# Norms of neighbourhood queries and keys: squares split in two parts, products made a piece at a time during the next block

## The chip, the cores and the metric

The kernel runs on one core of one Trainium2 chip. The core has five engines with a queue of instructions each: TensorE (PE in the profile; its weight loads are shown as PEld), VectorE (DVE), ScalarE (ACT), GpSimd (POOL) and SyncE (SP), which here issues nearly all DMAs. The metric is the device time of one execution in microseconds (us), less is better. The clock of TensorE that was granted in the profiled execution is 0.982 of full speed on average.

## The reference

One layer of a hybrid backbone over 1024 latent tokens of 1024 channels and 256 context tokens. After RMSNorm and modulation one input projection feeds two groups: a gated DeltaNet (conv blocks `q`, `k`, `v`, gate `z`; scans in both directions, which need the inverses of small triangular matrices) and a neighbourhood attention with 8 heads of 64 channels. Both outputs are joined, projected, and a SwiGLU network follows. The change touches only the norms of the attention group's queries and keys:

```python
q, k, v = [t.reshape(B, L, NA_HEADS, NA_HEAD_DIM) for t in jnp.split(p, 3, axis=-1)]
q = rms_norm(q, q_norm_w) * NA_HEAD_DIM ** -0.5
k = rms_norm(k, k_norm_w)
```

where `rms_norm` divides by the root of the mean of the squares over the 64 channels of a head (plus 1e-6) and multiplies by a weight per channel.

## The kernel before, in words

Tokens lie along the free axis: T = 1280, context first (`SEGS` cuts them in pieces of 256, 512 and 512; queries need the last two only, 1024 tokens). The input projection is made in blocks of 128 output channels. `Block` is such a block with the channels on the partitions: kinds `q`, `k`, `v` (conv), `nq` and `nk` (attention), four of each. `Wide` is a pair of blocks with the tokens on the partitions (`z`, `nv`), made in tiles of 128 tokens.

Products are three-term: inputs and weights are kept as a high part and the remainder, both in the type fp32r, which PE takes in one pass (`hh`, `hl`; `whi`, `wlo`), and high x high, low x high and high x low are added in PSUM (line 389). For one of the 8 contraction tiles (`KT`) and one term a block has as many matmuls as pieces. Matmuls on plain fp32 data are two instructions each in the trace.

The list `jobs` has the order: `k` 0 to 3 and `nv` half 1, then `nk` 0, 1, 2, `nv` half 0, `nk` 3, `nq` 0, 1, 2, `q` 0 to 3, `z`, `v` 0, `z`, `v` 1 to 3, `nq` 3. In round n of the loop (from line 974 on) the next job's weights are prefetched (a DMA, a cast to `whi` on ACT at line 198, a subtraction to `wlo` on POOL at line 199), job n's matmuls are made, its result is copied out of PSUM (`evac`, line 422 for `nq` and `nk`), then the norm of job n-1 is made (`norm`), and last the squares of job n (`silu`, line 455). Where job n is a `Wide`, the norm of job n-1 is made after its fifth tile.

The norm of an `nk` or `nq` block: for each piece a matmul of the squares `r` with a 128 x 128 matrix of two blocks of ones, `M[C_BD2]`, in plain fp32 (line 476), which sums the squares of a head and spreads the sum over its channels; Ln on ACT out of PSUM (line 477); after the pieces Exp with factor -0.5 (479 for `nq`, 481 for `nk`); a multiplication on DVE (484); a split into two fp16 parts on ACT and DVE (489, 490; 496, 497); four DMAs to DRAM (502). The matmul's result lies in a bank of the tag `m`, of which there are two; the banks of the blocks have the tag `blk`, of which there are four.

Between the contraction tiles and token tiles, `bg.step` runs background work a step at a time: first `block_inverses` (POOL makes `rc` at line 782, PE and ACT make `W` at 795 and 797, DVE multiplies at 802 to 807, PE transposes at 814, DVE eliminates at 824 and 826, PE turns back at 836, the result goes to DRAM as `x_d`), then `preps` (lines 886 to 920), which loads it as `xc`. The first four preps need the context chunks only; the others wait until the `q` blocks are done. From the job `nq` 3 on, attention starts (`sc`, lines 295 to 319), and the scans follow.

The order of instructions in each queue is not the written one: a planner takes the instructions in the written order but moves what its own estimate of times holds ready ahead of what it holds late, and allocates buffers of a tag in turn. A queue works strictly in the order so fixed. The tag `kx` has three buffers of up to 1280 x 4 bytes, used by `hl16`, `vt`, `kT`, `kk`, `kd` and the `z` tiles.

Of the kernel before, what the change touches and what calls it, by code (L numbers as in the profile page):

```python
# [9 lines left out]
F32 = mybir.dt.float32  # L10
F32R = mybir.dt.float32r
# [3 lines left out]
OP = mybir.AluOpType  # L15
# [4 lines left out]
D, L, CT, T = 1024, 1024, 256, 1280  # L20
# [13 lines left out]
C_ID, C_LE, C_GE, C_BD2, C_ONE = range(5)  # L34
# [53 lines left out]
def hybrid(ctx, tc, a, dbg):  # L88
    nc = tc.nc
    pe, act, dve, pool, sp = nc.tensor, nc.scalar, nc.vector, nc.gpsimd, nc.sync  # L90

    def pools(stack, name, side=None, bufs=1, **kw):
        if side:
            kw["side"] = side
        return stack.enter_context(tc.tile_pool(name=name, bufs=bufs, reuse_waits="tile", **kw))
# [19 lines left out]
    def const(name, shape, dt=F32):  # L115
        return mid.tile(shape, dt, name=name, tag=name)
# [5 lines left out]
    M = [cst[:, i * 128:(i + 1) * 128] for i in range(4)] + [ones]  # L122
# [12 lines left out]
    for i, v in enumerate((EPS, -0.5 * math.log(64.0))):  # L135
        dve.memset(bias[:, i:i + 1], v)
    b_eps, b_naq = bias[:, 0:1], bias[:, 1:2]
    mr = const("mr", [128, 5, 128], F32R)
    mneg = const("mneg", [128, 2, 128], F32R)

    v_d = dram.tile([T, 512], F32, name="v_d", tag="v_d")
# [218 lines left out]
    with ExitStack() as bs:  # L360
# [7 lines left out]
        def bank(name="m"):  # L368

            if len(psum) == 1:  # L370
                return psum[0].tile([128, 512], F32, name=name, tag="ps")
            return psum[1].tile([128, 512], F32, name=name, tag=name, bufs=4 if name == "blk" else 2)
# [19 lines left out]
        class Block:  # L392
# [56 lines left out]
            def silu(self):  # L449
                acc, t0 = self.acc, self.t0  # L450
                if self.kind in "qkv":
                    act.activation(acc[:, t0:], acc[:, t0:], AF.Silu)
                if self.kind in ("q", "nq", "nk"):
                    self.r = cp.tile([128, T], F32, name="cr", tag="cr", bufs=2)
                    act.activation(self.r[:, t0:], acc[:, t0:], AF.Square)

            def norm(self):

                kind, acc, t0, i = self.kind, self.acc, self.t0, self.i
                if kind == "v":  # L460
                    return
                if kind == "k":
                    sp.dma_start(kT_d[:, i], acc)
                    return
                r = self.r
                if kind == "q":
                    sp.dma_start(qT_d[:, i], acc[:, t0:])
                    p = bank()
                    for c in range(8):
                        pe.matmul(p[:, c:c + 1], r[:, t0 + c * 128:t0 + (c + 1) * 128], M[C_ONE][:, 0:1],  # L470
                                  start=True, stop=True)
                    dve.tensor_copy(SQ[:, :, i], p[:, 0:8])
                    return
                for s0, n in self.segs:
                    p = bank()
                    pe.matmul(p[:, :n], M[C_BD2], r[:, s0:s0 + n], start=True, stop=True)
                    act.activation(r[:, s0:s0 + n], p[:, :n], AF.Ln, bias=b_eps, scale=1.0 / ND)
                if kind == "nq":
                    act.activation(r[:, t0:], r[:, t0:], AF.Exp, scale=-0.5, bias=b_naq)
                else:  # L480
                    act.activation(r[:, t0:], r[:, t0:], AF.Exp, scale=-0.5)
                isk = kind == "nk"
                u = acc
                dve.scalar_tensor_tensor(u[:, t0:], u[:, t0:], qkw[:, isk:isk + 1], r[:, t0:],
                                         op0=OP.mult, op1=OP.mult)
                hl16 = cp.tile([128, 2, T], F16, name="hl16", tag="kx", bufs=3)
                h16, l16 = hl16[:, 0], hl16[:, 1]
                if isk:
                    act.copy(h16, u)
                    dve.tensor_tensor(l16, u, h16, OP.subtract)  # L490
                else:
                    for hf in range(2):
                        s = slice(t0 + hf * 512, t0 + hf * 512 + 512)
                        uv = u[:, s].rearrange("p (r b c) -> p b r c", r=8, b=4)
                        hv, lv = (x[:, s].rearrange("p (b r c) -> p b r c", b=4, r=8) for x in (h16, l16))
                        act.copy(hv, uv)
                        dve.tensor_tensor(lv, uv, hv, OP.subtract)
                for i, x in enumerate((h16, l16)):
                    for hb in range(2):
                        hd = 2 * self.i + hb  # L500
                        dst = nk_d[i, hd] if isk else nq_d[hd, i]
                        sp.dma_start(dst, x[hb * 64:hb * 64 + 64, t0:])
# [99 lines left out]
        with ExitStack() as xs:  # L602
# [13 lines left out]
            for k in range(KT):  # L616
                x = xp.tile([128, T], F32, name=f"xt{k}", tag=f"xt{k}")
# [12 lines left out]
            pool.memset(wide, 0.0)  # L630
            pool.tensor_copy(wide[:, :, 0:2], sc2)
            pool.tensor_copy(mr[:, 4], ident)
            for d in range(2):
                pool.tensor_scalar(mneg[:, d], masks[:, d], -1.0e30, None, op0=OP.mult)
            pool.tensor_copy(mr[:, 0:4], masks)
# [34 lines left out]
            for s0, n in SEGS:  # L670
                p = bank()
# [28 lines left out]
        cp = pools(bs, "cp", "right")  # L700
# [262 lines left out]
        def blk(n):  # L963
            return jobs[n] if 0 <= n < len(jobs) and isinstance(jobs[n], Block) else None
# [9 lines left out]
        for n in range(2, len(jobs) + 2):  # L974
            j = jobs[n] if n < len(jobs) else None
            if n == inv:
                bg2.drain()
                bg2s.close()
                early.close()
                psum.append(bs.enter_context(tc.tile_pool(name="psa", bufs=1, space=PSUM)))  # L980
                bg.add(block_inverses())
                bg.add(preps())
            if n == len(jobs) - 1:
                bg.drain()
                late.close()
                fill = attention(pools(attn, "nw", "left", 2))
                next(fill)
            if n + 1 < len(jobs):
                jobs[n + 1].prefetch()
            fin = blk(n - 2) if n - 2 not in done else None  # L990
            fin = fin.finish() if fin else iter(())
            nrm = blk(n - 1)
            if isinstance(j, Wide):
                for t, _ in enumerate(j.tiles()):
                    next(fin, 0)
                    if t == 4 and nrm:
                        nrm.norm()
                        for _ in fin:
                            pass
                        fin = nrm.finish()  # L1000
                        done.add(n - 1)
                        nrm = None
                    bg2.step(2)
                    if n < turn:
                        bg.step(2)
                    if n >= turn:
                        bg.step(5)
            elif j:
                for k in range(KT):
                    j.mm([k])  # L1010
                    if k >= 3:
                        next(fin, 0)
                    bg.step(1 if n < turn else 3)
                    bg2.step(1)
                j.evac()
            for _ in fin:
                pass
            done.add(n - 2)
            if isinstance(j, Wide) and n == values:
                vlat = nv_d[CT:].rearrange("(r c) d -> r c d", c=64)  # L1020
                for cb in range(4):
                    for ch in range(4):
                        sp.dma_start(vw_d[:, cb, ch], vlat[4 * ch:4 * ch + 4, BLKS[cb]:BLKS[cb] + 32])
            if nrm:
                nrm.norm()
            if isinstance(j, Block):
                j.silu()
# [176 lines left out]
    nrm = pools(early_u, "nrm", "left")  # L1204
# [16 lines left out]
    class Stream:  # L1221
# [67 lines left out]
        def next(self, n=2):  # L1289

            while len(self.got) < n:
                self.make()
            out = [self.got.pop(0) for _ in range(n)]
            return out
# [21 lines left out]
    with ExitStack() as os_:  # L1316
# [3 lines left out]
        for k in range(4):  # L1320
            raw = wp.tile([128, KT, 132], F32, name="wraw", tag="wraw", bufs=2)[:, :, :128]
            sp.dma_start(raw, na_d[k].rearrange("p (i t) -> p i t", t=128))
            n = nap.tile([128, 2, L], F32R, name=f"na{k}", tag=f"na{k}")
# [18 lines left out]
        for b in range(KT - 2):  # L1342
# [3 lines left out]
            for k in range(KT):  # L1346
                for j, (wi, xi) in enumerate(((0, 0), (0, 1), (1, 0))):
                    for o, s in zip(outs, HV):
                        pe.matmul(o, w[wi][:, k], parts[xi][k][:, s], start=k == 0 and j == 0,  # L1349
                                  stop=k == KT - 1 and j == 2)  # L1350
# [14 lines left out]
        for t, s in enumerate(HV):  # L1365
            outs = [bank(), bank()]
            last.append(outs)
            for k in range(KT):
                for j, (wi, xi) in enumerate(((0, 0), (0, 1), (1, 0))):
                    for o, w in zip(outs, ws):  # L1370
                        pe.matmul(o, w[wi][:, k], parts[xi][k][:, s], start=k == 0 and j == 0,  # L1371
                                  stop=k == KT - 1 and j == 2)
# [183 lines left out]
    for n, (wn, xn) in enumerate(zip(Stream.DOWN, FACTORS)):  # L1556
        o = chains[n in (1, 3, 5)]
        for p in range(NFB // 2):
# [4 lines left out]
            for j, b in order:  # L1563
                wi, xi = ((0, 0), (0, 1), (1, 0))[j]
                pe.matmul(o[b], w[wi][:, b], F[xn, p][xi], start=n in (0, 1, 5) and p == 0 and j == 0,  # L1565
                          stop=p == NFB // 2 - 1 and j == 2, skip_group_check=True)
# [3 lines left out]
        for b in range(4):  # L1570
            x = out[i, t][b]
# [74 lines left out]
```

## Time and profile before

| | us |
|---|---|
| median of 3 runs | 1607.62 |
| lowest and highest | 1607.45, 1609.95 |
| the profiled execution | 1608.33 |
| its span, first to last instruction | 1606.5 |
| from its start to the first `nk` norm's products (line 476) | 193.1 |
| to the last `nq` norm's products | 610.4 |

A row of the timeline reads: start in us, duration in us, engine, line, operation, output<-inputs, shape, count; in brackets the idle time of the engine just before and what ended it. A row can merge several instructions that follow each other, and durations of matmuls overlap, so the distance between starts is what PE gives to a row. In rows by groups, the figures behind the bar are busy time and mean duration in ns, and then idle time before.

### The profile page before, as it was taken

The numbers are of one execution on the slowest core, as the hardware profiler recorded it, in microseconds if no ns is written. First come the engines' busy times: TensorE is split into PE (matmuls) and PEld (weight loads), VectorE is DVE, ScalarE is ACT, GpSimd is POOL, SyncE is SP. The second block draws the span as 40 slices with busy tenths as digits, with TensorE's granted clock in tenths as the row PEclk, the third lists the DMA queues.
The fourth block names the chain that finished last, engine by engine and source line by source line (L and its number), as shares of the span: only waits on it lengthen the run. The fifth ranks groups of instructions, "written<-read, shape, count | busy, mean of one in ns | idle before, by whom it ended". The sixth has DMA issues, their size and how long they took to land.

```text
span 1606.5 us, 24016 instructions
## 1 busy us (share of the span) xinstructions
PE 1504.8 (94%) x8594; PEld 1265.4 (79%) x8594; DVE 1037.5 (65%) x1934; ACT 713.9 (44%) x1348; POOL 201.2 (13%) x275
## 2 busy tenths in 40 slices
PE   3999899899999998998997999999999999999999
PEld 1689788678888876787785887888888888888887
DVE  5866588445365665677897449865665655679752
ACT  5342452664434316666674147333333333544441
POOL 2053600512243310000000000000000000000000
PEclk9999999999999998999998999999999999999999
DMA  9366133535545348999846811532232333698742
GB/s 371 125 198 204 57 91 139 181 102 164 164 134 185 99 133 252 284 299 284 247 147 201 277 40 40 190 105 99 103 108 101 116 108 112 229 368 298 260 153 85
DMA packets 211529, 275.23 MB, mean 171 GB/s; under 512 B 15953, under 2 KB 119889, under 8 KB 210385
## 3 DMA queue, kind: packets, MB, share of 16 engines
q1 hardware_dynamic: 210544, 273.06, 52.2%
q8 instruction: 68, 1.11, 0.3%
q10 hardware_dynamic: 864, 0.63, 0.1%
q14 instruction: 53, 0.43, 0.1%
HBM read 206.78 MB, written 71.04 MB: 173 GB/s over the span
## 4 chain that ended last, share of the span: by engine, by line
PE 75%; DVE 7%; DMA 7%; ACT 5%; issue 3%; POOL 2%; SPq 1%; ACTq 0%; DVEq 0%; POOLq 0%
PE ps L1218 26%; PE ps L1565 13%; PE blk L389 10%; PE ps L1349 3%; PE blk L572 3%; PE pr L919 3%; PE sc L317 3%; PE sc L307 2%; PE sc L295 2%; PE pr L910 1%; PE ps L1111 1%; DVE tt L824 1%; PE ps L1371 1%; DMA nv_d<-zt 1%; DMA fraw<-w_conv 1%
## 5 line engine op out<-in xcount | busy, mean ns | idle before, releaser
L389 PE MATMUL blk<-hh,whi 128*128 128x512 f32 (+1 forms) x416 | 125.4, 394 | 4.1 <-ACT whi L198 1.6
L1279 ACT CAST uhi<-ws 128x512 fp32r<-128x512 f32 x91 | 54.7, 622 | 151.2 <-PE ps L1218 76.8
L1279 ACT CAST uhi<-wq 128x512 fp32r<-128x512 f32 x101 | 60.6, 621 | 135.9 <-issue 61.3
L389 PE MATMUL blk<-hh,wlo 128*128 128x512 f32 (+1 forms) x416 | 117.8, 377 | 2.3 <-POOL wlo L199 2.3
L389 PE MATMUL blk<-hl,whi 128*128 128x512 f32 (+1 forms) x416 | 115.5, 375 | 0.0
L1280 DVE TENSOR_TENSOR ulo<-wq,uhi 128x512 fp32r<-128x512 f32 x101 | 67.5, 688 | 66.9 <-ACT uhi L1279 36.9
L1218 PE MATMUL ps<-hT,uhi 128*128 128x512 f32 x336 | 104.3, 392 | 3.1 <-ACT hT L1397 3.1
L1218 PE MATMUL ps<-lT,uhi 128*128 128x512 f32 x336 | 103.6, 390 | 0.0
L1218 PE MATMUL ps<-hT,ulo 128*128 128x512 f32 x336 | 103.5, 389 | 0.0
L1218 PE MATMUL ps<-hB,uhi 128*128 128x512 f32 x288 | 89.7, 392 | 0.0
L1218 PE MATMUL ps<-lB,uhi 128*128 128x512 f32 x288 | 89.2, 391 | 0.0
L1218 PE MATMUL ps<-hB,ulo 128*128 128x512 f32 x288 | 88.9, 389 | 0.0
L389 PEld LDWEIGHTS blk<-hh,wlo 128*128 128x128 f32 x416 | 73.1, 191 | 18.3 <-POOL wlo L199 2.9
L389 PEld LDWEIGHTS blk<-hh,whi 128*128 128x128 f32 x416 | 71.6, 195 | 18.9 <-issue 3.2
L1280 DVE TENSOR_TENSOR ulo<-ws,uhi 128x512 fp32r<-128x512 f32 x91 | 60.8, 687 | 37.5 <-ACT uhi L1279 29.2
L389 PEld LDWEIGHTS blk<-hl,whi 128*128 128x128 f32 x416 | 73.4, 192 | 13.6 <-DVE hl L689 0.3
L572 PE MATMUL blk<-zhi,hh 128*128 128x264 f32 (+1 forms) x288 | 83.9, 291 | 0.0
L572 PE MATMUL blk<-zhi,hl 128*128 128x264 f32 (+1 forms) x288 | 82.1, 285 | 0.0
L572 PE MATMUL blk<-zlo,hh 128*128 128x264 f32 (+1 forms) x288 | 81.7, 284 | 0.0
L198 ACT CAST whi<-wraw 128x1024 fp32r<-128x1024 f32 x26 | 27.3, 1049 | 121.0 <-PE blk L389 50.3
L1218 PEld LDWEIGHTS ps<-hT,uhi 128*128 128x128 f32 x336 | 63.1, 189 | 16.4 <-ACT hT L1397 3.5
L1218 PEld LDWEIGHTS ps<-lT,uhi 128*128 128x128 f32 x336 | 63.4, 189 | 13.2
(333 smaller groups left out, 3738.5 us busy)
## 6 DMA issues: line engine op xcount, KB each, us to landing
wq<-w_fo SPq DMA_DIRECT2D x99, 256.0 KB
wq<-w_gu SPq DMA_DIRECT2D x88, 256.0 KB
wad<-wa SPq DMA_DIRECT2D x64, 256.0 KB
bt<-rpb SPq DMA_DIRECT2D x64, 192.0 KB
t_d<-g SPq DMA_DIRECT2D x22, 512.0 KB
fr<-t_d SPq DMA_DIRECT2D x44, 256.0 KB
f_d<-g SPq DMA_DIRECT2D x33, 256.0 KB
fr<-f_d SPq DMA_DIRECT2D x33, 256.0 KB
```

What stands on the lines that cost most here:

```text
L198: act.copy(h, r)
L295: pe.matmul(sc[:, u * 640 + n0:u * 640 + n1], q, ks[i], start=i == 0, stop=i == 1)
L307: pe.transpose(sc[:, u * 640 + j * 128:u * 640 + (j + 1) * 128], bt[:, j * 128:(j + 1) * 128], ident)
L317: pe.matmul(sc[u * ND:u * ND + ND, 1280:1408], vv, pt[:, j * 128:(j + 1) * 128], start=j == 0, stop=j == 4)
L389: pe.matmul(o, ww[:, k], xx[k][:, s], start=k == 0 and j == 0, stop=k == KT - 1 and j == end)
L572: pe.matmul(p[:, :c1 - c0], x[k][:, s], ww[:, k, c0:c1], start=k == 0 and j == 0, stop=k == KT - 1 and j == 2)
L919: pe.matmul(p[:, hs[h]], f[:, h], src[:, h], start=True, stop=True)
L1218: pe.matmul(o, w[wi][:, k], x[xi][:, k], start=first and k == 0 and j == 0, stop=k == n - 1 and j == 2, skip_group_check=True)
L1279: act.copy(hi, self.raw[key])
L1280: dve.tensor_tensor(lo, self.raw[key], hi.bitcast(F32), OP.subtract)
L1349: pe.matmul(o, w[wi][:, k], parts[xi][k][:, s], start=k == 0 and j == 0, stop=k == KT - 1 and j == 2)
L1565: pe.matmul(o[b], w[wi][:, b], F[xn, p][xi], start=n in (0, 1, 5) and p == 0 and j == 0, stop=p == NFB // 2 - 1 and j == 2, skip_group_che ...
```

## The change

The squares of an `nq` or `nk` block are split like the other operands: `rh` is a cast of `r` to fp32r on ACT, `rl` the remainder, made on POOL; both are written right after the squares, in buffers of the tag `kx`. The matrix of ones is cast to fp32r once at the start (`mr[:, 5]`, on POOL). For each piece the norm makes two one-pass matmuls, with `rh` and `rl`, in place of one in fp32.

The norm becomes a generator, `norming`, that pauses after each piece. If job n is a `Block`, the norm of an `nq` or `nk` job n-1 is no longer made after job n's matmuls and copies out of PSUM, but among them: one piece after each contraction tile from the fifth on, then the rest (Exp, multiplication, split, DMAs). For `nk` the rest follows after the eighth tile, for `nq` after the seventh. Where job n is a `Wide` (for `nk` 2), or there is none (for `nq` 3), the place stays as it was and the norm is made at one go.

```diff
                 if self.kind in ("q", "nq", "nk"):
                     self.r = cp.tile([128, T], F32, name="cr", tag="cr", bufs=2)
                     act.activation(self.r[:, t0:], acc[:, t0:], AF.Square)
+                if self.kind in ("nq", "nk"):
+                    self.rh = cp.tile([128, T], F32R, name="rh", tag="kx", bufs=3)
+                    act.copy(self.rh[:, t0:], self.r[:, t0:])
+                    self.rl = cp.tile([128, T], F32R, name="rl", tag="kx", bufs=3)
+                    pool.tensor_tensor(self.rl[:, t0:], self.r[:, t0:], self.rh[:, t0:].bitcast(F32), OP.subtract)
 
             def norm(self):
+
+                for _ in self.norming():
+                    pass
+
+            def norming(self):
...
                 for s0, n in self.segs:
                     p = bank()
-                    pe.matmul(p[:, :n], M[C_BD2], r[:, s0:s0 + n], start=True, stop=True)
+                    for j, x in enumerate((self.rh, self.rl)):
+                        pe.matmul(p[:, :n], mr[:, 5], x[:, s0:s0 + n], start=j == 0, stop=j == 1)
                     act.activation(r[:, s0:s0 + n], p[:, :n], AF.Ln, bias=b_eps, scale=1.0 / ND)
+                    yield
...
             pool.tensor_copy(mr[:, 4], ident)
+            pool.tensor_copy(mr[:, 5], M[C_BD2])
...
             elif j:
+                early_norm = iter(())
+                if nrm and nrm.kind in ("nq", "nk"):
+                    early_norm, nrm = nrm.norming(), None
                 for k in range(KT):
                     j.mm([k])
+                    if k >= 4:
+                        next(early_norm, 0)
                     if k >= 3:
                         next(fin, 0)
                     bg.step(1 if n < turn else 3)
                     bg2.step(1)
+                for _ in early_norm:
+                    pass
                 j.evac()
```

More of the change, by code (lines that the diff above doesn't have):

```diff
@@ L137, in hybrid @@
     b_eps, b_naq = bias[:, 0:1], bias[:, 1:2]
-    mr = const("mr", [128, 5, 128], F32R)
+    mr = const("mr", [128, 6, 128], F32R)
     mneg = const("mneg", [128, 2, 128], F32R)
```

## The prediction

> **What bounds the kernel now.** I read the page first, then the chain of work in order of time for the stage that the change touches, then the waits of TensorE there, and only then single rows.
>
> ```profile
> span 1606.5 us, 24016 instructions
> PE 1504.8 (94%) x8594; PEld 1265.4 (79%) x8594; DVE 1037.5 (65%) x1934; ACT 713.9 (44%) x1348; POOL 201.2 (13%) x275
> ...
> PE 75%; DVE 7%; DMA 7%; ACT 5%; issue 3%; POOL 2%; SPq 1%; ACTq 0%; DVEq 0%; POOLq 0%
> ```
>
> By the average, PE is the bound, and an edit that takes work from PE should pay. But the edit lies in one stage, from 175 us (end of the first `nk` block) to 352 us (norm of the third `nq` block), and there the chain is mixed:
>
> ```profile
> 177.23 3.30 POOL rc L782 x2
> ...
> 181.71 2.29 POOL rc L782
> ...
> 186.43 1.16 POOL rc L782 x2
> ...
> 271.31 0.51 DVE N L826
> ...
> 272.54 0.53 PE m L836 x2
> ...
> 292.33 4.96 DMA xc<-x_d
> ```
>
> This is the background work, the block inverses: POOL makes the products `rc` (line 782), DVE eliminates (824 and 826), PE turns the result back (836), it goes through DRAM and lands as `xc` for the first `preps`. PE waits for this chain, beside its waits in the norms:
>
> ```profile
> PE m L476 <- ACT cr L477: 5.1, 4, 1.5
> ...
> PE m L836 <- DVE N L830: 3.2, 1, 3.2
> ```
>
> (Columns: total us, times, longest.) The reader is to see two things of like size: the stall that the change attacks, 5.1 us over the four `nk` norms, and a stall of 3.2 us in which PE is already too early for the inverses. Whatever makes PE faster ahead of 272 us lengthens the second.
>
> **What the products cost now, and after.** The norm of `nk` block 0, on PE:
>
> ```profile
> 192.52 0.75 PE L389 MATMUL blk<-hh,wlo 128*128 128x256 f32 x3
> 193.11 1.45 PE L476 MATMUL m<-cr,cst 128*128 128x256 f32 x4
> 194.00 0.68 PE L389 MATMUL blk<-hh,whi 128*128 128x256 f32 x1
> 196.05 1.12 PE L476 MATMUL m<-cr,cst 128*128 128x512 f32 x2 [1.37 <-ACT cr L477]
> 196.61 1.03 PE L389 MATMUL blk<-hh,whi 128*128 128x512 f32 x2
> 197.48 0.73 PE L389 MATMUL blk<-hl,whi 128*128 128x256 f32 x3
> ```
>
> A one-pass round over 1280 tokens takes 0.59 us (192.52 to 193.11). From 193.11 to 197.48 are 4.37 us with one such round in them: the norm costs PE 3.78 us, 1.37 of them waiting for the Ln that frees a bank. After the change it is two rounds, 1.2 us, so 2.6 us go; four `nk` blocks: 10.4 us. An `nq` norm has only two pieces and no wait:
>
> ```profile
> 337.90 0.62 PE L389 MATMUL blk<-hh,wlo 128*128 128x512 f32 x2
> 338.36 1.88 PE L476 MATMUL m<-cr,cst 128*128 128x512 f32 x4
> ...
> 340.55 0.62 PE L389 MATMUL blk<-hl,whi 128*128 128x512 f32 x2
> ```
>
> 2.19 us less one round of 0.46 is 1.73, after it 0.91: 0.8 us each, 2.5 us for `nq` 0 to 2. PE is relieved of 12.9 us in all. `nq` 3 comes when PE has nothing else; see the end of the stage.
>
> **What the chain of inverses pays.** The added instructions are a cast on ACT and a subtraction on POOL for each of the eight blocks. Their nearest rows, and those of DVE that they meet:
>
> ```profile
> L538 POOL TENSOR_TENSOR kd<-kk,cst 128x1280 f32<-128x1280 f32 x1 | 2.9, 2919 | 13.4 <-ACT nA L716 13.4
> ```
> ```profile
> 165.75 1.05 POOL L782 TENSOR_TENSOR rc<-GH,cst 128x512 fp32r<-128x512 f32 x1 [3.35 <-DVE gY L746]
> ...
> 215.22 2.51 POOL L199 TENSOR_TENSOR wlo<-wraw,whi 128x1024 fp32r<-128x1024 f32 x1 [13.50 <-ACT whi L198]
> ```
> ```profile
> 191.15 3.59 DVE L802 TENSOR_TENSOR W<-W,NB 128x1280 f32<-128x1280 f32 x1 [8.06 <-ACT W L797]
> ...
> 196.30 1.49 DVE L805 TENSOR_TENSOR W<-W,WK 128x1280 f32<-128x1280 f32 x1
> 197.83 1.51 DVE L807 STREAM_TRANSPOSE WK<-W 128x1280 f32<-128x1280 f32 x1
> ...
> 215.55 2.82 DVE L824 TENSOR_TENSOR tt<-N 80x600 f32<-80x600 f32 x1
> 218.41 0.78 DVE L826 TENSOR_TENSOR N<-N,tt 80x600 f32<-80x600 f32 x1
> ```
>
> Block 0's subtraction (2.9 us) becomes ready about 178, in the middle of POOL's `rc` queue, which the chain runs through: +2.9 (between 0, if it finds the gap after the last `rc`, and 2.9). POOL and DVE get in each other's way: the `rc` that takes 1.05 alone takes 2.29 at 181.71, and the DVE step of 0.78 takes 2.82 while POOL subtracts, 2.0 lost to a POOL instruction of 2.5. At that ratio one of 2.9 us costs a DVE chain 2.4. Block 1's falls at about 199 to 202, when by then the delayed `W` steps still run: +2.4; block 2's falls into the elimination, where DVE is hardly ever idle: +2.4 (each between 0 and 2.9). Block 3's comes after the elimination: 0.
>
> [...]
>
> Tables: the norm of block 0 moves to the fifth to eighth step of block 1, among the exponentials of line 797, which run at present without reloading:
>
> ```profile
> 190.74 0.38 ACT L797 ACTIVATE W<-m 128x256 f32<-128x256 f32 x1
> ...
> 194.22 1.28 ACT L477 ACT_TABLE_LOAD   x1
> 195.52 0.47 ACT L477 ACTIVATE cr<-m,bias 128x256 f32<-128x256 f32 x1
> ```
>
> One Exp reload ahead of the last line 797 adds 1.3 (between 0 and 2.6, for a Ln and an Exp table). [...]
>
> Against this stands a slack: PE takes the transposes of `W` at 200.40, and the last DVE step ends at 199.34.
>
> ```profile
> 200.40 1.03 PE L814 MATMUL m<-cst,WK 128*80 128x128 f32 x8
> ```
>
> So the chain grows by 2.9 + 2.4 + 2.4 + 1.3 - 1.1 = 7.9 us up to PE's line 836 and the first `preps` behind it.
>
> **What PE has done by then.** The order of each queue is fixed beforehand by the planner, which moves ready work ahead of late work. Where it knows that PE's norm is cheaper, it puts more products ahead of line 836; what it doesn't see, PE waits away. It does not see the table load: it puts the third norm product one product behind the second, where Ln is 1.37 us late. So I let it know the products' own saving, 2.6 - 1.4 = 1.2 for each of four `nk` norms, 4.8 us (between 0 and 10.4). The norms of `nq` 0 to 2 lie beside or behind the first `preps` and give their 2.5 in full.
>
> **The end of the stage.** `nq` 3's squares go to the norm with nothing beside them, and attention's first scores wait for its Ln:
>
> ```profile
> 609.30 1.06 ACT L455 ACTIVATE cr<-cacc 128x1024 f32<-128x1024 f32 x1
> 610.38 1.28 ACT L477 ACT_TABLE_LOAD   x1
> 611.67 1.45 ACT L477 ACTIVATE cr<-m,bias 128x512 f32<-128x512 f32 x2
> ```
> ```profile
> 613.17 0.27 PE L295 MATMUL sc<-kh,qs 128*128 128x256 f16 x1 [0.78 <-ACT cr L477]
> ```
> ```profile
> 615.62 1.28 DVE L484 SCALAR_TENSOR_TENSOR cacc<-cacc,qkw,cr 128x1024 f32<-128x1024 f32 x1 [0.66 <-ACT cr L479]
> ```
>
> Now Square ends at 610.36 and Ln starts at 611.67, with the table load between. After: a cast (1.06, as Square), the subtraction (2.5), a pair of products (0.46) stand there, 4.0 us, of which the load covers 1.3: Ln is 2.7 later (between 0, if the order puts the scores first, and 2.7). DVE's line 484 waits for that Ln's Exp, and attention's steps queue behind it.
>
> Edits at nothing: the cast of the block matrix on POOL lies in the opening wait for inputs; eight casts on ACT lie beside PE (ACT is busy 44%), without that cover up to 1 us each; in `nq` 0 the pair lies among `preps` and could cost up to 3. The three `kx` buffers are reused a block later, so I expect no wait. `hl16`'s four stores move some 3 us earlier in SP's queue, past no load that waits for them. Evacuation loses the norm's products as cover; at 194.00 the next block gets one product in before it, so up to 0.7 once.
>
> **The sum.** +7.9 - 4.8 - 2.5 + 2.7 = +3.3 us on the profiled execution's 1608.33: **1611.6**. That execution is 0.7 above the median of 1607.62; the bound of 0.2%, which is about what a measurement of this kernel can tell from no change, lies at 1604.4 and 1610.8.
>
> **Rivals.** *Faster*: POOL's subtractions slip into idle stretches and PE stays the bound. For it: POOL is 13% busy. Against it: the busy stretch is just where the first lands. With chain growth z the result is 1608.33 + z - 4.6, so below z = 0.7 it is faster than 0.2%; with none and all 10.4 us of `nk` kept, 12.9 - 2.7 = 10.2 less, 1598; middle 1602. *No change to tell*: z between 0.7 and 7.1, about 1608. *Slower by another way*: PE reaches a low-part product before POOL has made it. POOL's `rc` queue speaks for it at block 0 only; 3 us there and the upper ends of chain and `nq` 0 (z about 14) give 1618.
>
> **Chances.** Forecast 0.40, faster 0.29, no change 0.23, the other slow way 0.08: faster 0.29, same 0.23, slower 0.48. The range cuts the outer tenth on each side: 1600 to 1618. The forecast's own: 1610.8 to 1616.
>
> **What would show it.** Right: the stall of line 476 gone; a 1280-wide subtraction among the `rc` rows; line 836's wait for DVE grown from 3.2 to some 6 or more; the elimination ending 5 to 8 us later against its start of the stage; the first scores 2 to 3 us later after the last product of the blocks. Wrong: line 836 no later than before relative to the stage's start, or PE finishing the `q` blocks 8 us or more earlier; then the time is near the faster rival.

## The result and the profile after

The changed kernel takes 1627.43 us (median of 4 runs, 1625.02 to 1629.53) against 1607.81 for the kernel before on the same chip: a ratio of 1.012, 95% interval 1.0102 to 1.0138. It is slower by 19.6 us. The forecast was slower by 3.3, and the range ended at 1618.

The page of the changed kernel, its first lines and the shares of the chain:

```profile
span 1627.6 us, 24045 instructions
...
PE 1510.3 (93%) x8594; PEld 1273.4 (78%) x8594; DVE 1044.2 (64%) x1934; ACT 723.8 (44%) x1356; POOL 229.4 (14%) x284
...
PE 73%; DVE 9%; DMA 6%; ACT 6%; POOL 3%; issue 3%; SPq 0%; ACTq 0%; DVEq 0%; POOLq 0%
```

POOL has 28 us more work and remains the least busy of the engines, at 14%; PE's work grew by 5.5 us although the norms' products are cheaper. Averages show little of what happened. The stage does. Busy time and granted clock (PEclk) in three stretches, first of the kernel before, then of the changed one. They begin with PE's first gate products (`pg`), in block `nk` 0; the marks between are the end of the elimination and the start of block `q` 0; the end is attention's first scores:

```profile
166.30:273.40 107.10, 97.39 (x580) 83.11 (x579) 81.10 (x77) 47.06 (x70) 28.40 (x18) 1.00 0.28 88
273.40:339.70 66.30, 58.48 (x311) 46.47 (x309) 24.52 (x35) 37.83 (x67) 25.78 (x46) 0.98 0.48 159
339.70:613.20 273.50, 259.60 (x1651) 229.58 (x1650) 152.77 (x226) 114.34 (x193) 77.83 (x98) 0.98 0.47 146
```
```profile
169.80:289.80 120.00, 102.01 (x589) 88.73 (x588) 83.56 (x76) 54.78 (x76) 41.81 (x21) 0.92 0.26 86
289.80:355.70 65.90, 58.70 (x300) 48.36 (x299) 27.19 (x36) 40.48 (x69) 32.43 (x47) 0.89 0.45 146
355.70:635.40 279.70, 260.53 (x1651) 230.74 (x1650) 153.00 (x226) 113.65 (x193) 82.89 (x100) 0.97 0.47 147
```

(Length, then busy time of PE, PEld, DVE, ACT and POOL, clock, DMA share, GB/s.) The first stretch is 12.9 us longer, the second 0.4 shorter, the third 6.2 longer: 18.7 in all. PE's busy time in the three together rises from 415.5 to 421.2, by 5.8; its idle time, length less busy, from 31.4 to 44.4, by 12.9. Busy time grew although the products are cheaper; what fell is the clock, to 0.92 and 0.89 in the first two stretches, where it had been 1.00 and 0.98. (Of the span's 21.1 us the rest is 3.5 ahead of the first mark and -1.1 behind the last.)

Where the idle time is, by PE's waits between 150 and 365 us of the changed kernel (total, times, longest, in us):

```profile
PE m L849 <- DVE N L843: 9.3, 1, 9.3
PE m L487 <- ACT cr L488: 4.0, 2, 2.1
PE m L487 <- POOL rl L460: 3.9, 2, 2.3
PE m L808 <- POOL rc L795: 3.8, 3, 1.9
```

Line 849 is the former 836: its wait for the elimination grew from 3.2 to 9.3. Line 487 is the former 476: the stall of 5.1 became 4.0 on Ln and 3.9 on the new low part. Line 808 is the product of `rc` (before 795).

How it begins, in block `nk` 1. POOL, ACT and PE of the changed kernel:

```profile
185.28 2.29 POOL L795 TENSOR_TENSOR rc<-GL,cst 128x512 fp32r<-128x512 f32 x1
187.53 2.96 POOL L460 TENSOR_TENSOR rl<-cr,rh 128x1280 fp32r<-128x1280 f32 x1
190.44 2.44 POOL L577 TENSOR_TENSOR zlo<-wraw,zhi 128x1056 fp32r<-128x1056 f32 x1
192.81 0.64 POOL L795 TENSOR_TENSOR rc<-GH,cst 128x256 fp32r<-128x256 f32 x1
```
```profile
196.18 1.08 ACT L576 CAST zhi<-wraw 128x1056 fp32r<-128x1056 f32 x1 [7.43 <-DMA wraw<-w_nv]
197.27 1.28 ACT L488 ACT_TABLE_LOAD   x1
...
199.06 1.28 ACT L810 ACT_TABLE_LOAD   x1
200.35 0.38 ACT L810 ACTIVATE W<-m 128x256 f32<-128x256 f32 x1
200.75 1.28 ACT L488 ACT_TABLE_LOAD   x1
```
```profile
187.62 0.50 PE L808 MATMUL m<-rc,mr 128*128 128x512 f32 x1 [1.75 <-POOL rc L795]
...
193.51 0.39 PE L808 MATMUL m<-rc,mr 128*128 128x256 f32 x1 [1.86 <-POOL rc L795]
...
199.09 0.80 PE L487 MATMUL m<-rh,mr 128*128 128x512 f32 x1 [1.82 <-ACT cr L488]
...
201.18 1.27 PE L389 MATMUL blk<-hl,whi 128*128 128x256 f32 x3
```

The subtraction stands in POOL's queue ahead of the last `rc`, and also ahead of `zlo`, the low part of `nv`'s weights. Only when `zlo` has read the buffer `wraw` does the next load of raw weights start: `zlo` ends at 192.88, the load is issued at 192.91. ACT therefore stands idle for 7.43 us until it can make that load's cast (4.58 in the kernel before), and `nk` 0's Ln and the last `W` of the inverses are queued behind the cast. Then ACT loads tables three times, twice ahead of the last `W` and once behind it. Block `nk` 1 takes 28.9 us from its first product to that of `nk` 2, where it had taken 20.2. And a round of products that takes PE 0.59 us at 192.52 in the kernel before starts 1.07 us ahead of the next at 201.18, where the granted clock is 0.50.

The end of the stage, from the last block product on (before: 608.16 to 613.17, 5.0 us; now 8.2):

```profile
627.15 1.04 PE L523 MATMUL m<-cst,cacc 128*128 128x128 f32 x8
...
629.19 1.65 DVE L527 TENSOR_TENSOR vt<-m,SV 128x512 f32<-128x512 f32 x3 [3.88 <-DMA v_d<-vt]
...
630.51 2.38 POOL L460 TENSOR_TENSOR rl<-cr,rh 128x1024 fp32r<-128x1024 f32 x1 [34.28 <-DVE vt L527]
...
632.94 0.80 PE L487 MATMUL m<-rl,mr 128*128 128x512 f32 x1 [1.85 <-POOL rl L460]
...
635.36 0.37 PE L295 MATMUL sc<-kh,qs 128*128 128x256 f16 x1 [0.78 <-ACT cr L488]
```

### The profile page after: what moved, and what is told of

Its sections match the earlier page's. It is cut to its first block, busy times and chain, and to the rows that moved or that the text cites. A ratio compares the mean times of both kernels' runs of the same rounds, so it can differ in the third digit from the quotient of the medians.

```text
span 1627.6 us, 24045 instructions
## 1 busy us (share of the span) xinstructions
PE 1510.3 (93%) x8594; PEld 1273.4 (78%) x8594; DVE 1044.2 (64%) x1934; ACT 723.8 (44%) x1356; POOL 229.4 (14%) x284
## 4 chain that ended last, share of the span: by engine, by line
PE 73%; DVE 9%; DMA 6%; ACT 6%; POOL 3%; issue 3%; SPq 0%; ACTq 0%; DVEq 0%; POOLq 0%
PE ps L1238 26%; PE ps L1585 13%; PE blk L389 10%; PE ps L1369 3%; PE pr L932 3%; PE blk L584 3%; PE sc L317 2%; DVE tt L837 2%; PE sc L307 2%; PE sc L295 2%; PE pr L923 1%; DVE N L839 1%; PE ps L1131 1%; DMA nv_d<-zt 1%; PE ps L1391 1%
## 5 line engine op out<-in xcount | busy, mean ns | idle before, releaser
L389 PE MATMUL blk<-hh,wlo 128*128 128x512 f32 (+1 forms) x416 | 122.1, 387 | 2.3 <-POOL wlo L199 2.3
L389 PE MATMUL blk<-hl,whi 128*128 128x512 f32 (+1 forms) x416 | 119.0, 383 | 0.0
L1238 PEld LDWEIGHTS ps<-hT,ulo 128*128 128x128 f32 x336 | 63.1, 188 | 13.1
```

The costliest lines, as they stand in the source:

```text
L389: pe.matmul(o, ww[:, k], xx[k][:, s], start=k == 0 and j == 0, stop=k == KT - 1 and j == end)
L1238: pe.matmul(o, w[wi][:, k], x[xi][:, k], start=first and k == 0 and j == 0, stop=k == n - 1 and j == 2, skip_group_check=True)
```

## The experiments

Every ratio is to the kernel before on the same chip. My theory was that of the prediction: POOL's subtractions lengthen the chain of inverses, and what PE saves is waited away. The main rivals were the new place of the norm, and the reordering by the planner that an edit can bring.

**The change taken apart.** The split alone, with the norm at its old place:

```diff
-                if nrm and nrm.kind in ("nq", "nk"):
-                    early_norm, nrm = nrm.norming(), None
```

> The squares are split and the products are one-pass as in the change, but the norm stays where it was, after the next block's matmuls. Theory 1 (the subtractions on POOL, with all that they delay in POOL's and ACT's queues, lengthen the chain of the block inverses): most of the 20 us stays, 1620 to 1626. Theory 2 (the new place: Ln and Exp behind late casts and among other exponentials, and PE at a low-part product that POOL has not made): 1604 to 1611, since POOL's work alone would cost only my 2.9 and the two meetings with DVE, less the cheaper products.

Measured: 1622.69 us, 1.0077 (1.0051 to 1.0103), as by theory 1. The move alone, with the fp32 product and without the split:

```diff
-                if self.kind in ("nq", "nk"):
-                    self.rh = ...
-                    self.rl = ...
...
-                    for j, x in enumerate((self.rh, self.rl)):
-                        pe.matmul(p[:, :n], mr[:, 5], x[:, s0:s0 + n], start=j == 0, stop=j == 1)
+                    pe.matmul(p[:, :n], M[C_BD2], r[:, s0:s0 + n], start=True, stop=True)
```

> The norm moves among the next block's matmuls as in the change, but the product stays one in fp32 and nothing is split: no cast, no subtraction. Theory 1: 1600 to 1606, faster than before by the stall of 5.1 us that goes. Theory 2: the new place costs by itself, 1614 to 1622.

Measured: 1616.18, 1.0048 (1.0032 to 1.0063), as by theory 2. Each half costs by itself. That the ratios add up to the whole (1.0125 against 1.012) says little: the move alone makes the long fp32 product in the new place, which the change doesn't make, and with a cheap product the new place costs little, as the last experiment shows. The change with the subtraction on DVE:

```diff
-                    pool.tensor_tensor(self.rl[:, t0:], ...
+                    dve.tensor_tensor(self.rl[:, t0:], ...
```

> The change with the subtraction on DVE in place of POOL. Theory 1: POOL's queue is as before, and DVE pays some 1.5 us a block, so about 1608 to 1616. Theory 2: the low part is made at about the same time and the norm sits at the same place, 1620 to 1628.

Measured: 1620.22, 1.0072 (1.0048 to 1.0096). Line 836's wait is 2.4 there, and the eight subtractions take 1.5 us at the median on DVE against 2.8 on POOL. So the way over POOL is dearer than adding the work to DVE itself, which the chain of inverses needs. But the result lies in theory 2's range: with no subtraction on POOL 0.72 of the 1.2% stay, and block `nk` 1 still takes 26.4 us. The loss is thus not POOL's alone; how it is divided there between DVE's added work and the norm's place I did not separate.

**The added work without its use.** To the kernel before I added the cast and the subtraction, read by nothing:

```diff
                     act.activation(self.r[:, t0:], acc[:, t0:], AF.Square)
+                if self.kind in ("nq", "nk"):
+                    self.rh = cp.tile([128, T], F32R, name="rh", tag="kx", bufs=3)
+                    act.copy(self.rh[:, t0:], self.r[:, t0:])
+                    self.rl = cp.tile([128, T], F32R, name="rl", tag="kx", bufs=3)
+                    pool.tensor_tensor(self.rl[:, t0:], self.r[:, t0:], self.rh[:, t0:].bitcast(F32), OP.subtract)
```

> The kernel before, with the cast to the high part and the subtraction of the low part for every nq and nk block added, and nobody reads them: products, place and order of the norm are as before. It measures the added work by itself. Theory 1: 1618 to 1626, the whole loss or more, as nothing is saved on PE. Theory 2: 1608 to 1614.

Measured: 1626.38, 1.0106 (1.0081 to 1.0131): as by theory 1, and most of the loss with none of the rest of the change. Without the two `rl` lines, so with the cast alone:

> The kernel before, with only the cast to the high part on ACT added for all eight blocks, read by nobody; no subtraction on POOL. The cast and the subtraction together cost 17 us. If POOL's subtraction is the cause: 1608 to 1612. If ACT's queue or the buffers of the tag kx are: 1616 to 1624.

Measured: 1609.78, 1.0005 (0.999 to 1.0021). The casts together cost nothing that shows, as forecast; the cost is the subtraction on POOL with its buffer. Then by place, `kind == "nk"` alone, `kind == "nq"` alone, and `kind == "nk" and i == 0` alone:

> The kernel before, with cast and subtraction added for the four nk blocks alone, read by nothing. With both added in all eight blocks it cost 17 us. Theory (each subtraction is paid where it falls: in the inverses' chain for nk 0 to 2, in the preps and at the end of the stage for nq): some +9, of it 4 in nk block 1, 4 to 5 more at line 836; tail before the first scores unchanged; 1615 to 1620. Rival (the order of the queues is rewritten by any added work, and that is what costs): about +14 or more here already, the nq blocks adding little.

> The kernel before, with cast and subtraction added for the four nq blocks alone, read by nothing. Theory: some +7, of it 3 to 4 between the last block product and the first scores and the rest among the preps; line 836 as before; 1613 to 1617; together with the run for nk about the 17 of both. Rival: the two runs do not add up to 17; this one then costs as much as both (over 12) or nothing.

> The kernel before, with cast and subtraction added for nk block 0 alone, read by nothing. Theory (the prediction's term of 2.9 was a good size for what POOL's queue loses, and this loss is carried to line 836): nk block 1 some 4 us longer, line 836 3 to 5 later, +3 to +5. Rival (one delay of the inverses is caught up by the slack of 1.1 us and by the order): 0 to +1.

Measured: for `nk` 1622.27, 1.0086 (1.0067 to 1.0105); for `nq` 1617.78, 1.0057 (1.0041 to 1.0072); for `nk` 0 alone 1614.02, 1.0044 (1.0029 to 1.0058). By the ratios that is 14, 9 and 7 us. Both kinds of place cost, and all three times lie above my theory's ranges. Added up, the two kinds come to more than both together, 1.0143 against 1.0106, a difference just outside the interval of the three runs taken together; whether they share part of their loss, and where, stays open. The rival of a rewritten order falls all the same: up to attention's first scores the traces of these three runs, of the cast alone and of the work in all eight blocks show on PE, ACT, DVE and POOL the same instructions in the same order as in the kernel before, apart from the added ones and ACT's table loads. With `nk` alone line 836 (here 841) waits, and with `nq` alone it doesn't; the first row below is of the former, the second of the latter:

```profile
PE m L841 <- DVE N L835: 7.9, 1, 7.9
```
```profile
PE m L841 <- DVE N L835: 3.2, 1, 3.2
```

The run with `nk` 0 alone shows the smallest unit, one POOL instruction of 2.96 us. First the product of `rc` on PE and the cast on ACT in the kernel before, then in this one, with the rounds that follow and two windows, before and after 191.7 us:

```profile
187.05 0.38 PE L795 MATMUL m<-rc,mr 128*128 128x256 f32 x1 [0.75 <-POOL rc L782]
...
189.76 1.07 ACT L564 CAST zhi<-wraw 128x1056 fp32r<-128x1056 f32 x1 [4.58 <-DMA wraw<-w_nv]
```
```profile
185.18 2.96 POOL L460 TENSOR_TENSOR rl<-cr,rh 128x1280 fp32r<-128x1280 f32 x1
...
191.13 0.38 PE L800 MATMUL m<-rc,mr 128*128 128x256 f32 x1 [3.63 <-POOL rc L787]
...
192.09 1.27 PE L389 MATMUL blk<-hh,whi 128*128 128x256 f32 x3
...
195.20 0.74 PE L389 MATMUL blk<-hh,whi 128*128 128x256 f32 x3
...
193.83 1.08 ACT L569 CAST zhi<-wraw 128x1056 fp32r<-128x1056 f32 x1 [7.42 <-DMA wraw<-w_nv]
```
```profile
187.50:191.10 3.60, 0.00 (x1) 0.00 (x0) 0.00 (x0) 0.00 (x0) 3.60 (x4) 1.00 0.00 0
191.70:195.20 3.50, 3.49 (x10) 2.97 (x11) 0.00 (x0) 1.36 (x2) 0.21 (x1) 0.52 0.38 139
```

PE's wait grows by 2.9 (0.75 to 3.63): the term of the prediction. Then the clock is 0.52 for 3.5 us: three rounds take 3.11 us, 192.09 to 195.20, instead of 3 x 0.59, another 1.3 to 1.4. Together this is nearly all of the 4.4 us by which block `nk` 1 is longer. The elimination ends 4.3 later against the first gate products, but line 836 waits 3.2 as before, since PE itself is late by as much. At block `q` 0 the delay is 6.2; the other 1.9 arise behind the elimination, where the clock is 0.91 in place of 0.98. In the run with the cast alone `q` 0 starts 2.4 later and the whole kernel is no slower, so those 1.9 need not be the subtraction's.

**The first block as before**, all else as in the change:

```diff
+                self.plain = self.kind == "nk" and self.i == 0
+                if self.kind in ("nq", "nk") and not self.plain:
...
+                if nrm and nrm.kind in ("nq", "nk") and not nrm.plain:
```

> The change, but nk block 0 keeps its fp32 product at its old place, without cast and subtraction; the other seven blocks are as in the change. By the traces the block nk 1, in which this norm falls, lost 8.8 us (4.4 by the added work, 4.0 by the new place). Theory A (the loss starts in that block and the chain of inverses hands it on): 7 to 11 us less than the change, 1617 to 1621. Theory B (each block costs about its part, some 2 us): 1624 to 1626.

Measured: 1624.88, 1.0085 (1.0063 to 1.0108). By its time this is theory B; by the ratios it is 5.6 us less than the change, between the two theories. Block `nk` 1 takes the time of before again (20.3 us against 20.2), but line 836 still waits 7.9 and some 14 us of loss stay: the other seven blocks suffice for them.

**What the products are worth.** The kernel before with one one-pass product for each piece, of squares that ACT writes in fp32r; cast, low part and subtraction are left out, and the place is the old one:

```diff
-                    act.activation(self.r[:, t0:], acc[:, t0:], AF.Square)
...
+                        act.activation(self.rh[:, t0:], acc[:, t0:], AF.Square)
...
-                    pe.matmul(p[:, :n], M[C_BD2], r[:, s0:s0 + n], start=True, stop=True)
+                    pe.matmul(p[:, :n], mr[:, 5], self.rh[:, s0:s0 + n], start=True, stop=True)
```

> The kernel before, with the square written by ACT as fp32r at once and one one-pass product of it: no subtraction, no more instructions on ACT, the norm at its old place. It leaves out the low part of the squares. It measures what cheaper products are worth where nothing is added. If PE were the bound of this stage: 1.7 us per product block and some of the wait, 10 us less, 1597 to 1600. If PE's gain ahead of line 836 is waited away there: 1602 to 1606.

Measured: 1608.28, 0.9995 (0.998 to 1.0011): cheaper products, with nothing added on POOL, gain nothing that shows, and neither of the expected times came. The gain is waited away, but not at line 836, where PE no longer waits at all. Ahead of `nk` 3 stands a wait that the kernel before doesn't have:

```profile
PE blk L389 <- ACT zt L587: 6.5, 1, 6.5
```

`zt` is ACT's copy of `nv` out of PSUM; in the kernel before such copies wait 6.3 us in three waits between 150 and 345 us for the store of `nv_d` to read their buffer, and I take this one to be of that kind. The planner's order is another one in this run; whether a third would keep the gain is not shown. And the stall taken away by itself, by a third bank for the third piece of an `nk` norm:

```diff
-                    p = bank()
+                    p = bank("pr" if s0 == 768 and len(self.segs) == 3 else "m")
```

> The kernel before, with the third piece of an nk norm in a free bank of the tag pr, so that the third product no longer waits for the first Ln; nothing else. It takes away the stall of 5.1 us that the change was after, with no added work. If the stall was worth its length: 1603 to 1605. If PE then only reaches line 836 and the first preps earlier and waits there: 1606 to 1609.

Measured: 1612.9, 1.0016 (1.0005 to 1.0028). The stall of 5.1 us is gone and the kernel is no faster, even slower by 0.16%, above both expected ranges. PE's waits at line 910, in the `preps`, in the kernel before, and then its waits between 150 and 370 us in this run:

```profile
PE pr L910 <- DVE kk L902: 3.8, 4, 1.9
...
PE pr L910 <- issue: 0.9, 1, 0.9
```
```profile
PE m L836 <- DVE N L830: 5.6, 1, 5.6
PE pr L910 <- DVE kk L902: 4.0, 1, 4.0
PE pr L910 <- issue: 3.4, 1, 3.4
```

Line 836 waits 5.6 in place of 3.2. In the `preps` behind it the waits for DVE come to 4.0 in place of 3.8, and the one for which the profile shows no releaser (`issue`) to 3.4 in place of 0.9. The three together are 5.1 longer: what PE gained it waits away. Where the 0.16% come from stays open.

**The new place without POOL.** The change with the single product of the rounded squares, so without cast, low part and subtraction:

> The change without its low part: Square writes the rounded squares directly, one one-pass product for each piece, no cast and no subtraction, norms at the new place. The mean squares are a rounded value's, so a part of the computation is left out. Theory (the new place costs by itself): as the move with the exact product, +5 to +9, 1613 to 1617, with the Ln of nk 0 held behind the cast that waits for the raw weights. Rival (the new place hurt only because of the long exact product and POOL's queue): no cost, 1606 to 1610.

Measured: 1610.52, 1.0011 (1.0 to 1.0023). My theory fell: the place by itself costs some 2 us, just at the edge of what the interval tells from nothing. With the added work's 1.0106 this comes to the change's 1.012. Most of the 7.5 us of the move with the exact product come with that product in the new place. Block `nk` 1 is 4.2 us longer there than here, and PE waits 2.9 for Ln in it; how the rest arises, I did not separate. The wait for `zt` tells nothing of it: it is 5.2 us in the move with the exact product and 5.4 in this run.

## Why the prediction was wrong, by its own steps

The direction and the main mechanism held: the subtraction of `nk` 0 stands among the `rc` rows, line 836 waits three times as long, the elimination ends later, and the scores start 3.2 us later after the last block product. One of the signs failed: line 487 still waits 4.0 us for Ln. And the sizes did not hold. Up to block `q` 0 the sum had 7.9 - 4.8 - 2.5 = 0.6 us; measured against the first gate products it is 12.5.

*The chain of inverses, +7.9.* This is the term that was mis-sized most. Against the first gate products the elimination starts 7.7 us later (221.16 less 169.8, before 210.01 less 166.3) and takes 5.4 longer (68.7 against 63.3), 13 in all.

Up to its start I had 2.9 + 2.4 + 1.3 - 1.1 = 5.5. The 2.9 for `nk` 0 is what PE's wait shows when that block is alone. But the step "in the middle of POOL's `rc` queue" looked at `rc` only and missed `zlo` in the same queue, which frees the one buffer of the next raw load, whose cast blocks ACT. Ahead of the last `W` it had one table load where there are two, and nothing of the clock. So ACT ends the last `W` 6.0 us later against the first gate products. The 2.4 for block 1 did not occur: its subtraction starts at 213.49, between the `W` steps and the elimination. A meeting of the kernel before even went away: the first `W` step on DVE, 3.59 us at 191.15 there beside POOL's `zlo`, takes 1.49 in the changed kernel. And the chain did not go through DVE there, as I had it. The last `W` step ends at 206.86, but PE makes the transposes only at 210.99, 4.1 later where it had been 1.1, since its own queue is late by then:

```profile
200.77 1.49 DVE L815 TENSOR_TENSOR W<-W,NB 128x1280 f32<-128x1280 f32 x1 [14.11 <-ACT W L810]
...
205.35 1.51 DVE L820 STREAM_TRANSPOSE WK<-W 128x1280 f32<-128x1280 f32 x1
```
```profile
210.99 1.04 PE L827 MATMUL m<-cst,WK 128*80 128x128 f32 x8
```

In the elimination I had one meeting of DVE with a subtraction, at 2.4. There are two, of blocks 2 and 3 (POOL is in them from 234.21 and from 277.67). DVE's line 824 (now 837) beside them, and the same shapes in the kernel before, without POOL:

```profile
235.73 3.72 DVE L837 TENSOR_TENSOR tt<-N 80x736 f32<-80x736 f32 x1
...
278.49 3.49 DVE L837 TENSOR_TENSOR tt<-N 80x672 f32<-80x672 f32 x1
```
```profile
221.00 0.92 DVE L824 TENSOR_TENSOR tt<-N 80x736 f32<-80x736 f32 x1
...
262.54 0.85 DVE L824 TENSOR_TENSOR tt<-N 80x672 f32<-80x672 f32 x1
```

They lose 2.8 and 2.6 us, together the 5.4 by which the elimination is longer. The size of a meeting was right, the number was not: "Block 3's comes after the elimination" misread the trace of before, where block 3's squares are made at 266.85 and the elimination ends at 273.3.

*What PE has done by then, -4.8, and the `nq` norms, -2.5.* These are the steps that failed outright. I saw that PE waits part of the gain away, and still gave 4.8 of 10.4 and all of 2.5. The run with cheaper products only is worth 0.05% with an interval around zero, and the run without the stall gains nothing either. In neither does a relief of PE ahead of line 836 count: it ends at the wait for `zt` in the one, at line 836 and in the `preps` in the other. Beside the added work the cheaper products may be worth more: the split at the old place is at 1.0077, the work without its use at 1.0106, but the intervals overlap. The `nq` norms did not give theirs "in full": in two of them PE waits 2.34 and 1.58 us for the low part, since the products of an `nq` block take only some 11 us (24 rounds of 0.46) and the fifth tile comes before POOL is done. That was the rival of the low part made too late, which I had put at `nk` 0; it occurred at `nq`.

*The end of the stage, +2.7.* It was 3.2. Cast, subtraction and products lie there as forecast: Ln starts 4.4 us after Square ends, where it had been 1.3. The step left out that the `kx` buffers are shared: `vt` waits 3.88 for a store of `v_d`. In the changed kernel this wait is over before the low part is ready, so it is not what the 0.5 above the forecast consist of. The run with `nq`'s work alone has the same wait, 3.87, and its end is 2.3 us longer, although nobody reads the subtraction; with the cast alone the end is 1.1 longer. The rest of the third stretch's 6.2 us lies almost all in the `q` blocks, 2.8 us, 1.58 of it the wait for `nq` 2's low part; the sum had nothing there.

*Edits at nothing.* The casts on ACT were nothing as a whole, as the cast-only run shows. "I expect no wait" for the `kx` buffers was wrong at `vt`. The pair of `nq` 0 among the `preps`, "up to 3", looked at one block of three and was too small a price for this place: with `nq`'s work alone block `q` 0 starts 7.2 us later, against 2.4 with the cast alone. What was taken as a row of single small costs on idle POOL was the largest cost of the change: 17 us in the run with the work alone. The cast of the matrix at the opening is no cost that shows: the run with cheaper products has it, and its first gate products start at 165.5, before 166.3. The changed kernel's 169.8 is therefore not explained by it; kernels without any change there begin between 165.8 and 169.0, and I leave it open how much of these 3.5 us belongs to the change.

*The rivals.* "POOL slips into idle stretches" is refuted by the work added without use: 17 us. The way to 1618 had the right ingredients and a price too low by 9.

## What to carry to other kernels

A small instruction on a nearly idle engine is priced by what is queued behind it there, not by the engine's share (here the run with one more of 2.96 us on POOL, 13% busy, was 7 us slower): follow its queue through to the buffer that it frees, the load that waits for that buffer, and the instruction that blocks another queue meanwhile. Before counting a gain on the busiest engine, look for the next place where that engine already waits for something else; if there is one, the gain can end there, as that of the stall's 5.1 us did here, and to take the stall away alone tests it cheaply. Adding the work of an edit to the old kernel without using it separates its price from its benefit in one run.

## What the runs showed of the hardware

I had not expected TensorE's clock in the sum. In the run with `nk` 0 alone it is 0.52 for 3.5 us behind a wait of 3.63 us, and in the changed kernel it is 0.50 from 188.0 to 191.4 and again from 194.8 to 205.1 us, with 1.00 between, where the only waits of over 1 us are 1.75, 1.86 and 1.82 long. The windows here are cut at other places, so they show means:

```profile
187.60:193.50 5.90, 4.03 (x12) 3.21 (x12) 0.00 (x0) 0.60 (x1) 5.90 (x4) 0.71 0.00 0
193.50:199.00 5.50, 3.57 (x11) 2.33 (x11) 0.00 (x0) 2.79 (x3) 2.19 (x2) 0.62 0.30 98
199.00:205.10 6.10, 6.01 (x16) 4.94 (x17) 4.26 (x3) 4.37 (x6) 0.74 (x1) 0.50 0.29 86
```

In the kernel before, with a wait of 1.75 us in the same place and then one of 0.75, it is 1.00 from 184.0 to 193.0. In the run with `nk` 0 alone the three rounds behind the wait took 3.11 us in place of 1.77, so the delay there is 1.3 us more than the 2.9 by which the wait itself grew. No run here tells what set off the half clock in either kernel.

The eight subtractions, four of 128 x 1280 and four of 128 x 1024, took 1.5 us at the median on DVE and 2.8 on POOL; one of 128 x 1280 took 2.96 on POOL in block `nk` 1 and 4.46 beside the elimination.
